# Contrast adjustment on one core: a split sixth load, and the first store moved from SyncE's queue to ScalarE's

## The chip, the cores and the metric

The kernel runs on one core of a Trainium2 chip. The metric is the time of one execution on the device in microseconds (us), lower is better. A core has five engines that run their own instruction streams: TensorE (PE in the profile), VectorE (DVE), ScalarE (ACT), GpSimd (POOL) and SyncE (SP). Data moves between the chip's memory (HBM) and the on-chip memory (SBUF, 128 partitions) by 16 DMA engines. A transfer is issued by an instruction on SyncE or ScalarE; the transfers that SyncE issues form one queue (q1 in the profile) and those that ScalarE issues another (q10), and every one of the 16 DMA engines works on both.

## The reference

The input is a batch of 16 pictures with 3 channels of 512x512 float32 values, 50.33 MB in all. Each channel picture has its own mean; values are pushed away from it by a factor of 1.5 and clipped to 0..1.

```python
batch, c, h, w = 16, 3, 512, 512
mean = np.mean(x, axis=(2, 3), keepdims=True)
return np.clip(mean + factor * (x - mean), 0, 1).astype(np.float32)
```

The formula is `factor * x + (1 - factor) * mean`, so a channel picture must be summed whole before its first value can be written.

## The kernel before

There are 48 channel pictures of 262,144 values. A picture is laid over 32 partitions of 8192 values each (`ROW`), so that a tile of 128 partitions holds four pictures and is 4.19 MB; there are 12 tiles, 0 to 11. All tiles live in a ring of `BUFS = 6` buffers, and a tile is changed in place: tile t uses buffer t modulo 6, so load t + 6 has to wait until store t has left the buffer.

For one tile the work is: one load (`load`, L63, on SyncE); `add` (L72), a copy in place on ScalarE that also sums each partition's row; `shift_by` (L77), a small matmul with a block matrix that adds the sums of 32 partitions and scales them, so that every partition holds the picture's shift in `bias`; `clip` (L83 and L87), two passes of VectorE, multiply and add, then maximum and minimum; and one store (`store`, L66), by default on ScalarE.

The order is written out by hand (`manual_schedule`): each engine takes its instructions in the order of the program, and the framework adds the waits that the data needs. It also gives every DMA one of eight semaphores, each used several times over; a DMA that takes over a semaphore may get a wait for the earlier DMA on it.

What sets the order around the change:

- SyncE issues loads 0 to 5 at once, without a wait. Then it issues store 0 in three pieces (`CUTS`: columns 0 to 1024, 1024 to 3072, 3072 to 8192), as soon as tile 0 has been clipped, then load 6 (which waits for all three pieces), load 7 (which waits for store 1), and so on to load 11.
- ScalarE sums tiles 0 to 4. Then comes a sum of the first 512 columns of tile 5 (`FIRST`), which waits until load 5 has landed. Because ScalarE works in order, this small sum is a gate: store 1 stands behind it in the program, then the sum of the other 7680 columns, then stores 2 to 4, store 5, and from there a sum and a store for each tile.
- So until load 5 has landed, no store of ScalarE's queue starts; the pieces of store 0 stand in SyncE's queue behind the six loads.

Below, "load 5" is the sixth load, "the gate" is the sum of 512 columns, and "piece 1, 2, 3" are the pieces of store 0.

Of the kernel before, what the change touches and what calls it, by code (L numbers as in the profile page):

```python
# [1 line left out]

# [4 lines left out]


P = 128  # L10
ROW = 8192
BUFS = 6
FIRST = 512
CUTS = (0, 1024, 3072, ROW)


@with_exitstack
def kernel(
    ctx: ExitStack,
    tc: tile.TileContext,  # L20
    x: bass.AP,
    factor: float,
    out: bass.AP,
):
    nc = tc.nc
    f32 = mybir.dt.float32
    Alu = mybir.AluOpType
    Act = mybir.ActivationFunctionType

    B, C, H, W = x.shape  # L30
    n_img, n_pix = B * C, H * W
    ppi = n_pix // ROW
    per_tile = P // ppi
    n_tiles = n_img // per_tile
    assert ppi * ROW == n_pix and per_tile * n_tiles == n_img and n_tiles > BUFS

    factor = float(factor)
    wconst = (1.0 - factor) / float(n_pix)

    x_f = x.rearrange("b c h w -> (b c h w)")  # L40
    out_f = out.rearrange("b c h w -> (b c h w)")

    def dram(ap, t, c0=0, c1=ROW):
        return bass.AP(tensor=ap.tensor, offset=t * P * ROW + c0, ap=[[ROW, P], [1, c1 - c0]])

    consts = ctx.enter_context(tc.tile_pool(name="consts", bufs=1))
    xpool = ctx.enter_context(tc.tile_pool(name="xpool", bufs=1))
    small = ctx.enter_context(tc.tile_pool(name="small", bufs=1))
    psum = ctx.enter_context(tc.tile_pool(name="psum", bufs=1, space=bass.MemoryType.PSUM))

    sums = small.tile([P, 2 * n_tiles], f32, name="sums")
    bias = psum.tile([P, n_tiles], f32, name="bias")


    blockw = consts.tile([P, P], f32, name="blockw")
    nc.gpsimd.memset(blockw, 0.0)  # L56
    for a in range(0, P, ppi):
        nc.gpsimd.memset(blockw[a : a + ppi, a : a + ppi], wconst)  # L58

    ring = xpool.tile([P, BUFS, ROW], f32, name="ring")  # L60

    def load(t):
        nc.sync.dma_start(out=ring[:, t % BUFS, :], in_=dram(x_f, t))  # L63

    def store(t, c0=0, c1=ROW, queue=nc.scalar):
        queue.dma_start(out=dram(out_f, t, c0, c1), in_=ring[:, t % BUFS, c0:c1])  # L66

    def add(t, c0=0, c1=ROW):
        part = ring[:, t % BUFS, c0:c1]
        k = 2 * t + (c0 > 0)  # L70
        own = sums[:, k : k + 1]
        nc.scalar.activation(out=part, in_=part, func=Act.Copy, accum_out=own)  # L72
        return own

    def shift_by(t, *parts):
        for k, part in enumerate(parts):
            nc.tensor.matmul(  # L77
                bias[:, t : t + 1], blockw, part, start=k == 0, stop=k == len(parts) - 1
            )

    def clip(t):
        part = ring[:, t % BUFS, :]
        nc.vector.tensor_scalar(  # L83
            out=part, in0=part, scalar1=factor, scalar2=bias[:, t : t + 1],
            op0=Alu.mult, op1=Alu.add,
        )
        nc.vector.tensor_scalar(  # L87
            out=part, in0=part, scalar1=0.0, scalar2=1.0, op0=Alu.max, op1=Alu.min
        )

    with tc.manual_schedule():
        for t in range(BUFS):
            load(t)

        gate = BUFS - 1
        for t in range(gate):
            shift_by(t, add(t))
            clip(t)  # L100
        for c0, c1 in zip(CUTS[:-1], CUTS[1:]):
            store(0, c0, c1, nc.sync)
        load(BUFS)
        first = add(gate, 0, FIRST)
        store(1)
        load(BUFS + 1)
        shift_by(gate, first, add(gate, FIRST))
        clip(gate)
        for t in range(2, gate):
            store(t)  # L110
            load(t + BUFS)
        for t in range(gate, n_tiles):
            if t > gate:
                shift_by(t, add(t))
                clip(t)
            store(t)
            if t + BUFS < n_tiles:
                load(t + BUFS)


# [1 line left out]
_INS = ['x', 'factor']  # L122
_OUTS = [((16, 3, 512, 512), 'float32')]

_NUMBERS = {'factor': 1.5}


# [26 lines left out]
```

## Time and profile before

| | |
|---|---|
| time, median of 3 runs | 239.94 us (239.68 to 240.33) |
| the profiled execution's own time | 239.92 us |
| its span, from the first to the last instruction | 238.1 us |
| moved by DMA | 100.66 MB, 423 GB/s over the span |
| VectorE busy | 107.0 us (45%) |
| ScalarE busy | 86.9 us (37%) |
| TensorE busy | 7.6 us (3%) |
| load 5 landed, gate ran | 62.06, 62.08 us |
| load 6 issued | 81.40 us |
| store 11 (the last) issued, landed | 220.07, 237.14 us |

The page gives the busy time of each engine, then the span in 40 slices of 5.95 us with the share in which the DMA engines were busy and the rate that they moved, then the queues, the chain of work that ended last, groups of instructions, and the DMA issues. The trace behind it has one record for each row of data that a DMA engine moved (start, duration, queue, bytes; 32,768 bytes is one partition of a whole tile, and an engine moves eight of them for a tile), and the times at which each DMA's semaphore was raised, which is what "landed" means here. Times in the text are counted from the start of the span, which is 1.8 us shorter than the execution's time.

### The profile page before, as it was taken

Reading aid. Unit: us, or ns where it says so; the run is one execution under the profiler, and the core shown is the slowest. Engines: PE = TensorE matmul, PEld = TensorE weight load, DVE = VectorE, ACT = ScalarE, POOL = GpSimd, SP = SyncE. Lnnn points to the kernel's source line nnn. Section 1 sums busy time; section 2 is a strip of 40 time slices with the busy share of each in tenths; the row PEclk is TensorE's granted clock in tenths of the full one; section 3 lists DMA queues with packets and bytes.
Section 4 is the critical chain, followed back from the end, with each engine's and each line's share of the span. In section 5 each row is a group of like instructions: output and inputs, shape, how many; then the busy total and the mean of one; then the engine's idle time right before and its main releaser. Section 6 shows DMA issues by size and latency. Waiting matters only on the chain.

```text
span 238.1 us, 209 instructions
## 1 busy us (share of the span) xinstructions
PE 7.6 (3%) x26; PEld 6.5 (3%) x26; DVE 107.0 (45%) x24; ACT 86.9 (37%) x27; POOL 0.9 (0%) x9
## 2 busy tenths in 40 slices
PE   0000000000100000000000000000000000000000
PEld 0000000000000000000000000000000000000000
DVE  0004988988979200000760490292094077059000
ACT  2085956959560000019007406503801900830000
POOL 1000000000000000000000000000000000000000
DMA  7999999999999999999999999999999999999995
GB/s 264 440 440 440 440 440 435 440 424 374 407 429 433 459 424 424 413 440 435 440 435 440 440 435 435 424 435 435 413 429 435 440 435 440 440 435 435 424 435 226
DMA packets 3744, 100.66 MB, mean 423 GB/s; under 512 B 416, under 2 KB 416, under 8 KB 544
## 3 DMA queue, kind: packets, MB, share of 16 engines
q1 hardware_dynamic: 2160, 54.53, 53.7%
q10 hardware_dynamic: 1584, 46.14, 44.9%
HBM read 50.33 MB, written 50.33 MB: 423 GB/s over the span
## 4 chain that ended last, share of the span: by engine, by line
DMA 55%; another core or an unknown queue 25%; DVE 4%; ACT 3%; issue 3%; SPq 1%; PE 0%
DMA ring<-in_x_dram 41%; DMA out_dram<-ring 15%; ACT ring L72 3%; DVE ring L83 2%; DVE ring L87 2%; SPq L63 1%; PE bias L77 0%
## 5 line engine op out<-in xcount | busy, mean ns | idle before, releaser
L72 ACT ACTIVATE ring<-ring 128x8192 f32<-128x8192 f32 (+2 forms) x13 | 84.5, 6503 | 122.7 <-DMA ring<-in_x_dram 122.7
L83 DVE TENSOR_SCALAR ring<-ring,bias 128x8192 f32<-128x8192 f32 x12 | 53.9, 4492 | 112.6 <-PE bias L77 112.6
L87 DVE TENSOR_SCALAR ring<-ring 128x8192 f32<-128x8192 f32 x12 | 53.1, 4427 | 0.4
L77 PE MATMUL bias<-sums,blockw 128*128 128x1 f32 x26 | 7.6, 360 | 203.5 <-ACT ring L72 198.8
L77 PEld LDWEIGHTS bias<-sums,blockw 128*128 128x128 f32 x26 | 6.5, 311 | 204.5 <-ACT ring L72 179.4
L72 ACT ACTIVATION_READ_ACCUMULATOR ring<-ring 128x1 f32 x13 | 2.4, 186 | 0.0
L72 ACT ACT_TABLE_LOAD x1 | 1.3, 1283 | 0.7 <-PEq L135 0.7
L58 POOL MEMSET blockw<- 32x32 f32 x4 | 0.5, 118 | 0.2
L56 POOL MEMSET blockw<- 128x128 f32 x1 | 0.2, 205 | 0.3 <-POOLq L135 0.3
L135 POOL MEMSET const-bfloat16-1.0<- 128x1 bf16 x1 | 0.1, 113 | 0.0
L135 POOL MEMSET const-uint8-127<- 128x1 uint8 x1 | 0.1, 113 | 0.0
L135 POOL MEMSET const-float32-1.0<- 128x1 f32 x1 | 0.1, 110 | 0.0
L135 POOL MEMSET const-float32-0.0<- 128x1 f32 x1 | 0.1, 104 | 0.2 <-issue 0.2
## 6 DMA issues: line engine op xcount, KB each, us to landing
ring<-in_x_dram SPq DMA_DIRECT2D x12, 4096.0 KB, 45.9
out_dram<-ring ACTq DMA_DIRECT2D x11, 4096.0 KB, 46.1
out_dram<-ring SPq DMA_DIRECT2D x1, 2560.0 KB, 50.6
out_dram<-ring SPq DMA_DIRECT2D x1, 1024.0 KB, 35.5
out_dram<-ring SPq DMA_DIRECT2D x1, 512.0 KB, 33.5
```

The costliest lines, as they stand in the source:

```text
L56: nc.gpsimd.memset(blockw, 0.0)
L58: nc.gpsimd.memset(blockw[a : a + ppi, a : a + ppi], wconst)
L63: nc.sync.dma_start(out=ring[:, t % BUFS, :], in_=dram(x_f, t))
L72: nc.scalar.activation(out=part, in_=part, func=Act.Copy, accum_out=own)
L77: nc.tensor.matmul(bias[:, t : t + 1], blockw, part, start=k == 0, stop=k == len(parts) - 1)
L83: nc.vector.tensor_scalar(out=part, in0=part, scalar1=factor, scalar2=bias[:, t : t + 1], op0=Alu.mult, op1=Alu.add,)
L87: nc.vector.tensor_scalar(out=part, in0=part, scalar1=0.0, scalar2=1.0, op0=Alu.max, op1=Alu.min)
L135: nc = _bacc.Bacc("TRN2", target_bir_lowering=False, num_devices=1)
```

## The change

The load of tile 5 becomes two DMAs, columns 0 to 6912 and columns 6912 to 8192 (`TAIL = 1280`), both on SyncE. The gate, which reads columns 0 to 512, then depends on the first part only. The three pieces of store 0 go from SyncE to ScalarE; there they stand behind the gate and ahead of store 1. SyncE goes from the loads of tile 5 directly to load 6, and all stores are on ScalarE's queue. The rest of tile 5 (columns 512 to 8192) waits for both parts.

```diff
+TAIL = 1280
 CUTS = (0, 1024, 3072, ROW)
...
-    def load(t):
-        nc.sync.dma_start(out=ring[:, t % BUFS, :], in_=dram(x_f, t))
+    def load(t, c0=0, c1=ROW):
+        nc.sync.dma_start(out=ring[:, t % BUFS, c0:c1], in_=dram(x_f, t, c0, c1))
 
-    def store(t, c0=0, c1=ROW, queue=nc.scalar):
-        queue.dma_start(out=dram(out_f, t, c0, c1), in_=ring[:, t % BUFS, c0:c1])
+    def store(t, c0=0, c1=ROW):
+        nc.scalar.dma_start(out=dram(out_f, t, c0, c1), in_=ring[:, t % BUFS, c0:c1])
...
     with tc.manual_schedule():
-        for t in range(BUFS):
-            load(t)
-
 
 
         gate = BUFS - 1
         for t in range(gate):
+            load(t)
+        load(gate, 0, ROW - TAIL)
+        load(gate, ROW - TAIL, ROW)
+
+        for t in range(gate):
             shift_by(t, add(t))
             clip(t)
+        first = add(gate, 0, FIRST)
         for c0, c1 in zip(CUTS[:-1], CUTS[1:]):
-            store(0, c0, c1, nc.sync)
+            store(0, c0, c1)
         load(BUFS)
-        first = add(gate, 0, FIRST)
         store(1)
         load(BUFS + 1)
         shift_by(gate, first, add(gate, FIRST))
```

More of the change, by code (lines that the diff above doesn't have):

```diff
@@ L91 @@
     with tc.manual_schedule():
-        for t in range(BUFS):
+        gate = BUFS - 1
+        for t in range(gate):
             load(t)
-        gate = BUFS - 1
+        load(gate, 0, ROW - TAIL)
+        load(gate, ROW - TAIL, ROW)
         for t in range(gate):
```

## The prediction, made before the changed kernel was built or run

> **What bounds the kernel now.** I read the slices of the page first:
>
> ```profile
> DMA  7999999999999999999999999999999999999995
> GB/s 264 440 440 440 440 440 435 440 424 374 407 429 433 459 424 424 413 440 435 440 435 440 440 435 435 424 435 435 413 429 435 440 435 440 440 435 435 424 435 226
> DMA packets 3744, 100.66 MB, mean 423 GB/s; under 512 B 416, under 2 KB 416, under 8 KB 544
> ```
>
> The DMA engines are busy from the first slice to the last; no engine of the core comes over 45%. So only three things can move the end: the start (264), the end (226), and the dip around 60 us (424, 374, 407), where the six loads run out and the stores begin. The change works on the dip alone.
>
> Next the DMA records of the trace. An engine moves a row of 32,768 bytes in 1.213 us, one of 20,480 in 0.761, one of 8192 in 0.309, one of 4096 in 0.158. A line through these is 0.0077 us + 0.0368 us per 1000 bytes. By it all rows of the kernel need 233.00 us on each of the 16 engines; the records add up to 234.58 us a engine, between 1.75 and 236.81 us. So there is hardly any idle time to win. The 1.58 us over the line lie at: the first rows of load 0 (0.69), the last two rows of load 5 (0.63, between 58 and 62 us), the entry of load 6 at 85 us (0.12) and what follows at 96 us (0.06); the remaining 0.08 are crumbs. A mean over engines:
>
> ```
> queue 1, data all moved      mean of 16 engines   last engine   landed
> load 4                              51.07            51.43       51.88
> load 5                              61.41            61.77       62.06
> piece 1 of store 0                  62.66            63.02       63.37
> ```
>
> Load 5 took 10.34 us after load 4 where eight rows need 9.70. The three pieces follow at once, since they had long stood behind it in the same queue:
>
> ```profile
> 0.75 2.88 SPq L63 DMA_DIRECT2D ring<-in_x_dram  x6
> 29.90 1.30 SPq L66 DMA_DIRECT2D out_dram<-ring  x3
> 81.40 74.34 SPq L63 DMA_DIRECT2D ring<-in_x_dram  x6
> ```
>
> Last ScalarE around the gate:
>
> ```profile
> 58.84 0.19 ACT L72 ACTIVATION_READ_ACCUMULATOR ring<-ring 128x1 f32 x1
> 62.08 0.63 ACT L72 ACTIVATE ring<-ring 128x512 f32<-128x512 f32 x1 [3.06 <-DMA ring<-in_x_dram]
> 62.09 1.49 ACTq L66 DMA_DIRECT2D out_dram<-ring  x2
> ```
>
> ScalarE is free from 59.03 us, the gate starts 0.02 us after load 5 has landed, and the first DMA behind it is issued 0.01 us later, while the gate still computes. So an issue behind the gate follows the landing by 0.03 us.
>
> **The change part by part**, against the profiled execution (239.92 us; the median of three is 239.94, so the sum holds for both).
>
> The split load. One more issue on SyncE, 0.37 to 0.53 us by those of loads 0 to 5, done by about 4.1 us; load 1 alone keeps the queue fed to 22 us, so it costs nothing. Eight rows an engine become 16: 8 x 0.0077 = 0.06, and a completion record of 0.01: +0.07 us on the bound.
>
> SyncE loses three issues (1.30 us at 29.90): nothing waits for SyncE there, so 0. The stall that they make at the end of load 5 goes with them, if my reading is right that the stores queued directly behind it stretch its last two rows (no other load, each with a load behind it, shows this; no run shows it alone). -0.63 us.
>
> When the first store can start now. The first part ends on the mean engine at 51.07 + 8 x 1.025 + 0.01 = 59.28 and on the last at 59.64; load 4, with a load behind it, landed 0.45 after its last engine, load 1 0.35: say 60.05. ScalarE is free (a cover of 1.0 us: if the sum of tile 4 ended later than 60.05, the gap below would grow one for one). Piece 1 is issued at 60.08. The second part ends on the mean engine at 59.28 + 8 x 0.196 + 0.01 = 60.86.
>
> From issue to first row there are three rows. At the start, with idle engines, load 0 was issued at 0.75 and its first rows began at 1.94 on average: 1.19. Store 1 was issued at 62.09 and began at 65.68 (3.6), load 6 at 81.40 and began at 85.50 (4.1), both into engines busy with the other queue. If an engine holds some 64 KB of rows already fetched (as the two stretched rows of load 5 suggest), these two become 1.1 and 1.65 us, since that much of the other queue was moved ahead of them. Piece 1 comes when only 0.8 us of small rows are left, so the start of the kernel is nearest: 1.19, first rows at 61.27, a gap of 61.27 - 60.86 = 0.41 us; 0.87 with 1.65.
>
> The first row after a gap. At the start it was stretched by 0.69 us; piece 1, following without a gap, by nothing. A queue that starts afresh is nearer to the first: +0.69, bounds 0 and 0.69.
>
> The Trainium skill, "DMA: Bandwidth & Descriptors", section "Latency and other measured facts", gives about 600 ns for the first byte of a DMA from these queues; by it the first row stands ready at 60.68, before the second part is through, and there would be no gap. The trace's own 1.19 us is what I use.
>
> ScalarE's new work. Three issues (0.348, 0.435 and 0.432 on SyncE; up to 1.06 as stores 2 and 3 took) put store 1 at 61.3 to 63.3 instead of 62.09, but its turn comes after the pieces' 1.27 + 2.47 + 6.09 = 9.8 us, near 71.8. The sum of the other columns of tile 5 moves by at most 1.6 us, its clip from 79.03 to at most 80.7; store 5 has no turn before about 144, when stores 2 to 4 are through. Cost 0.
>
> The order of transfers. Store 0 now has the engines to itself: it lands near 72.5 instead of 81.39, load 6 is issued then, and with the 4.1 us of before its rows begin at 76.4 to 76.6, not 85.50. Loads and stores then alternate, 19.4 us for a load. Store 1 has 3.8 rows out by then, the other 4.2 take 10.2 us, it lands at 88.2 (81.58 before), and load 7 is issued; load 6 keeps queue 1 fed to 95.8, so 7.6 us of cover. Were it gone, queue 10 would use the engines alone. Load 11 lands near 194 instead of 203.27, and store 11 is ready 16.8 us later, at 211, with its turn at about 226.5: 15 us of cover, 5.8 before. The bytes are the same and a row takes 1.213 us in mixed and in pure stretches, so 0. The stretches at 85 and 96 (0.18) I expect again at the new entry of load 6.
>
> Sum: +0.07 - 0.63 + 0.41 + 0.69 = +0.54, so 240.46, say 240.5 us. Bounds of the same mechanism: 0.07 - 0.63 + 0.41 = -0.15 and 0.07 - 0.63 + 0.87 + 0.69 = +1.00; and if the stretched rows remain with a small gap, 0.07 + 0.41 + 0.3 = 0.8.
>
> **The rivals.**
>
> *On time, and faster.* Piece 1's rows are ready when the second part ends on each engine: that takes an issue-to-row time of 0.78 us or less. Then 0.07 - 0.63 = -0.56, 239.36; and if load 6 now joins without the 0.18 of stretches, 239.18, which is over 0.3% faster. For it: the pieces are small rows, quick to fetch, and issue gets going while the engines are still warm. Against it: the only row with idle engines has 1.19.
>
> *Long start.* A queue that starts beside a busy one needs the 3.6 us of store 1 as such, not for what was fetched ahead. First rows at 63.7, gap 2.8, sum 0.07 - 0.63 + 2.8 = +2.3 to +2.9 with the stretch: 242.2 to 242.8. For it: both rows with a busy engine. Against: the engines are busy only 0.8 us more, and the two agree with the start's once rows fetched ahead are allowed for.
>
> *The gate opens late.* Piece 1 takes over a semaphore whose earlier DMA is the second part, and waits for its landing (61.22 + 0.42 = 61.64), or the first part lands late. The trace of before shows such waits: store 6 went out at 125.89 when load 7 had landed at 125.82, though its clip ended at 123.23. Then the first row is at 61.67 + 1.19 = 62.86, the gap 2.0, the sum 0.07 - 0.63 + 2.0 + 0.69 = +2.1: 242.0. Against: seven loads leave one of eight semaphores unused for piece 1.
>
> The Trainium skill, same page, section "Anatomy of one DMA — SWDGE (gpsimd) path", puts the fixed cost of a DMA at about 2.0 us, most of it the receipt from the target memory; with 2 us after 59.64 the gate would open at 61.64 as well, and the time would be 242.0. The trace's 0.29 to 0.45 us from last row to landing speaks against it, and I add nothing to this case for it.
>
> *Nothing.* The stretched rows have another cause and stay, and there is no gap: +0.07, 240.0. The same page, section "Issuing engines are not separate DMA queues", says that which engine issues changes nothing but issue time, which here would be this case. The trace agrees in that a row takes 1.213 us in either queue.
>
> **How the numbers follow.** 0.3% is 0.72 us, about what a measurement can tell here (the three runs span 0.65 us); slower starts at 240.66, faster below 239.22. Chances: the sum's case 0.60 (own range 239.8 to 241.0; 0.25 of it beyond 240.66), long start 0.14, late gate 0.11, on time 0.11 (0.07 beyond 239.22), nothing 0.04. Slower 0.25 + 0.14 + 0.11 = 0.50; faster 0.07; within 0.35 + 0.04 + 0.04 = 0.43. The range 239.5 to 242.3 leaves out the on-time case (0.11) and the upper half of the long start (0.07).
>
> **What would show it.** Gate near 60.07, piece 1 issued at once behind it; idle DMA engines or stretched rows between 60.9 and 62; load 5's rows at 1.025 without stretch; load 6 issued near 72.5; load 11 landed near 194; no stretch of idle DMA after that. Wrong would be: piece 1 issued after 61.5 (late gate), its first rows after 63 (long start), or before 61 (on time).

## The result, and the profile after

| | before | after |
|---|---|---|
| time, median of 5 runs | 239.94 us (239.68 to 240.33) | 241.21 us (241.02 to 241.34) |
| ratio to before, 95% interval | | 1.0053 (1.0038 to 1.0067) |
| profiled execution, its span | 239.92, 238.1 us | 241.28, 239.2 us |

The change makes the kernel slower by 1.27 us (0.53%). The forecast was 240.5 us in a range of 239.5 to 242.3, with 0.50 on slower. The direction and the range hold, but the sum behind the forecast (+0.54) is less than half of what came, and two of its terms were wrong in opposite directions.

The slices of the changed kernel's page, 5.98 us each:

```profile
DMA  7999999999999999999999999999999999999996
GB/s 263 438 438 438 438 438 438 438 397 414 438 416 351 438 427 427 438 433 416 411 427 438 438 438 438 433 433 438 427 438 438 438 438 438 433 427 405 427 433 263
```

The DMA engines are as busy as before. The deepest dip, though, is no longer the end of the loads. That was 424, 374, 407 and is now 397, 414 (slices 9 and 10) and then 438. The new one is 351, in slice 13, from 71.8 to 77.7 us. That is where load 6 joins. Before, load 6 joined at 85 us, and its slice showed 424.

ScalarE around the gate, start and duration in us (ACTq is its issuing of DMAs):

```profile
58.83 0.19 ACT L73 ACTIVATION_READ_ACCUMULATOR ring<-ring 128x1 f32 x1
60.10 0.63 ACT L73 ACTIVATE ring<-ring 128x512 f32<-128x512 f32 x1 [1.08 <-DMA ring<-in_x_dram]
60.11 1.08 ACTq L67 DMA_DIRECT2D out_dram<-ring  x2
...
61.22 1.82 ACTq L67 DMA_DIRECT2D out_dram<-ring  x2
63.09 6.61 ACT L73 ACTIVATE ring<-ring 128x7680 f32<-128x7680 f32 x1 [2.26 <-issue]
...
71.63 16.91 SPq L64 DMA_DIRECT2D ring<-in_x_dram  x2
```

The gate runs at 60.10 and piece 1 is issued at 60.11, as the change intends. The last line is SyncE's: load 6 goes out at 71.63 instead of 81.40.

The DMA records tell where the time went. I call "stretch" what a row takes beyond its length's usual time (1.213 us for 32,768 bytes), summed and divided by the 16 engines; "idle" is likewise per engine.

```
us per engine                         before    after    difference
all rows at the usual time            233.00   233.06      +0.06
stretch of the first rows (0 to 20)     0.72     0.71      -0.01
stretch, rows begun at 57 to 67.9       0.63     0.19      -0.44
idle, 57 to 70                          0        0.13      +0.1 to 0.2
stretch, rows begun at 67.9 to 130      0.19     1.65      +1.46
end of the last row, mean of engines  235.94   237.24      +1.30
end of the last row, last engine      236.80   237.84      +1.04
time outside the span                   1.79     2.03      +0.24
```

The idle of "before" comes out at -0.08, the error of this sum, so the difference lies between 0.13 and 0.21. (The time outside the span is taken from the unrounded spans, 238.13 and 239.25 us.) At the change from loads to stores the new kernel wins about 0.2 us. It then loses 1.46 us around load 6's entry. Its 1.65 us of stretch there are 1.02 on rows begun at 74 to 78, 0.43 at 86 to 90, 0.10 at 92, and crumbs. The first of these are rows of the stores, begun at 74.6 to 74.8: about 3 us after load 6 was issued, and about 2 us before its own first row (76.52). Such a row stands on all 16 engines in the changed kernel, and on three of them in the kernel before (begun at 85.4 to 85.8). Why does the same load, joining the same kind of stores, cost more than eight times as much? The experiments are about that.

### The profile page after: what moved, and what is told of

Its sections match the earlier page's. It is cut to its first block, busy times and chain, and to the rows that moved or that the text cites. A ratio compares the mean times of both kernels' runs of the same rounds, so it can differ in the third digit from the quotient of the medians.

```text
span 239.2 us, 211 instructions
## 1 busy us (share of the span) xinstructions
PE 7.6 (3%) x26; PEld 6.5 (3%) x26; DVE 107.0 (45%) x24; ACT 87.0 (36%) x27; POOL 0.9 (0%) x9
## 4 chain that ended last, share of the span: by engine, by line
DMA 51%; another core or an unknown queue 24%; DVE 4%; issue 3%; ACT 3%; SPq 1%; ACTq 1%; PE 0%
DMA ring<-in_x_dram 32%; DMA out_dram<-ring 19%; ACT ring L73 3%; DVE ring L84 2%; DVE ring L88 2%; SPq L64 1%; ACTq L67 1%; PE bias L78 0%
```

## The experiments

All kernels were timed in five rounds against the kernel before. Times are medians, with the ratio to the kernel before and its 95% interval. Stretch, idle time and the times of rows are those of one profiled execution of each kernel. The medians of the kernel before in the three series were 239.81, 239.73 and 239.63 us.

### First series: the moment, or engines in lockstep?

Two theories. M, the moment: load 6 now joins earlier (near 76 instead of 85), alone and while VectorE works on tile 5. L, lockstep: the short idle gap lets all engines begin the pieces within 0.2 us of each other (0.6 us apart in the kernel before), so that load 6 hits all of them at once.

**Load 6 into buffer 1.**

```diff
+    def slot(t):
+        return {BUFS: 1, BUFS + 1: 0}.get(t, t % BUFS)
-        ... ring[:, t % BUFS, ...]
+        ... ring[:, slot(t), ...]
```

> The changed kernel, but load 6 goes into buffer 1 and load 7 into buffer 0, so that load 6 waits for store 1 instead of store 0. It should be issued near 81 us, with load 7 directly behind it, as in the kernel before, and not at 71.6. In the changed kernel the rows around load 6's entry were stretched by 1.55 us a engine (1.02 at 74 to 78 us, 0.43 at 86 to 90, 0.10 at 92); in the kernel before by 0.18. Theory M (the moment: load 6 joins store 1 early, alone, while VectorE clips tile 5): the stretches fall to about 0.2 and the time to 241.2 - 1.35 = 239.85 us. Theory L (lockstep: the short idle gap at 61 us makes all 16 engines start the pieces together, so that load 6's first rows meet on all of them): the stretches stay near 1.5 wherever load 6 joins, and the time at 241.2.

Measured: 240.32 us (ratio 1.0022, 1.0014 to 1.0031). This is not the experiment that I meant. Load 6 stands ahead of store 1 in the program, so with buffer 1 it did not wait for store 1 but overwrote tile 1 (which this kernel therefore never stores). SyncE issued it at 39.50 us, long before the gate, so that it followed load 5 without a pause:

```profile
39.50 42.37 SPq L67 DMA_DIRECT2D ring<-in_x_dram  x2
```

As a kernel with seven loads ahead of the stores it still says something. The rows at the end of load 5 were not stretched and no engine idled. The pieces began at 64.3 us beside load 6, whose last rows, at 68 to 71 us, were stretched by 0.4; about 0.5 came from 85 us on, where load 7 joins. The proper version is in the third series.

**A longer second part.**

```diff
-TAIL = 1280
+TAIL = 2048
```

> The changed kernel with the second part of load 5 at 2048 columns instead of 1280. The gate opens near 59.2 us and piece 1's rows come near 60.1, while the second part is still being moved, so no engine idles and the engines keep the 0.6 us by which their rows are apart. Theory L: load 6's entry costs about 0.2 and the time is near 239.7 to 239.9 us. Theory M: the entry still costs 1.5; only the gap of 0.2 goes: 241.0.

Measured: 241.85 us (1.0068, 1.005 to 1.0086). The gate in this kernel:

```profile
59.21 0.63 ACT L73 ACTIVATE ring<-ring 128x512 f32<-128x512 f32 x1 [0.19 <-DMA ring<-in_x_dram]
59.22 0.86 ACTq L67 DMA_DIRECT2D out_dram<-ring  x2
```

Both theories missed the time. The gate opened at 59.21 and no engine idled, yet the later stretch is 1.69. So the gap is not needed, and L as I had put it falls. The engines are less in step than in the changed kernel, but more than in the kernel before: at load 6's entry the rows of 14 of the 16 begin within 0.29 us (0.15 and 0.41). I come back to this below. The rest of the loss in the profiled execution (242.19 us) is two engines that end at 238.57 and 238.78, where the mean of the 16 is 236.91.

**The kernel before, store 4 first on ScalarE.**

```diff
         load(BUFS)
         first = add(gate, 0, FIRST)
+        store(4)
         store(1)
...
         for t in range(2, gate):
-            store(t)
+            if t != 4:
+                store(t)
             load(t + BUFS)
```

> The kernel before, but ScalarE issues store 4 first (it has to wait for its clip, 68.65 us), then stores 1, 2, 3. The pieces of store 0, still behind load 5 on SyncE's queue, then have the engines to themselves, store 0 lands near 72 instead of 81.4, and load 6 joins near 76 us beside store 4, with no idle gap at 61 us before. Theory M: the entry costs about 1.5 as in the changed kernel, and the time is 239.94 + 1.35 = 241.3 us. Theory L: the engines were never idle, the entry costs 0.2, and the time stays at 239.9.

Measured: 239.69 us (0.9999, 0.9988 to 1.001). The slices of this kernel, 5.95 us each, and from its timeline SyncE's issue of load 6:

```profile
GB/s 265 441 441 441 441 435 441 424 419 408 393 466 408 419 419 441 441 441 435 435 435 441 435 419 419 424 435 441 441 435 435 435 435 430 430 441 408 430 441 265
```

```profile
71.86 0.34 SPq L63 DMA_DIRECT2D ring<-in_x_dram  x1
```

Load 6 was issued at 71.86 us and its first rows began at 75.89, as early as in the changed kernel. Slices 12 and 13 together carry (466 + 408) / 2 = 437, with no hole (466 is more than the engines move anywhere else; rows seem to be booked in the slice where they begin, so the two are read together). The stretch at the entry is 0.07. An early entry alone costs nothing, so M as the mere moment falls. What was left of it was VectorE, which stood idle from 68.7 to 77.0 us here.

**The changed kernel without the split.**

```diff
-        load(gate, 0, ROW - TAIL)
-        load(gate, ROW - TAIL, ROW)
+        load(gate)
```

> The changed kernel without the split: load 5 is one DMA again, the gate waits for all of it, and the pieces are on ScalarE. The gate opens 1.57 us after where it did against the end of the load: landing near 61.6 us, piece 1's rows 0.9 us later near 62.5, idle 1.6 us more than in the changed kernel. Both theories: 241.2 + 1.5 = 242.7 us. The last two rows of load 5 on each engine should not be stretched (0.63 us in the kernel before), since no store stands behind them in the queue; if they are, the stretch has another cause and the time is 243.3.

Measured: 242.93 us (1.0128, 1.0113 to 1.0144); 242.7 was expected. Slices of this kernel, 6.04 us each:

```profile
GB/s 260 434 434 434 434 434 434 434 434 434 311 432 385 412 390 407 428 434 434 434 434 434 434 434 434 434 434 434 434 434 434 434 434 434 434 434 434 434 434 184
```

The move alone costs 3.1 us; 311 is the idle gap. The engines idle 1.69 us, and the later stretch is 1.62. The rows of load 5 take 1.217 us on average, so they are not stretched: the 0.63 us of the kernel before do come from stores that wait behind the load.

### Second series: VectorE, or a queue that has gone empty?

Theory V: VectorE's passes over tile 5, at 70 to 79 us, hinder the entry. Theory Q: SyncE's queue had stood empty for 15 us, and a queue that starts afresh costs this.

**No clip of tile 5.**

```diff
         shift_by(gate, first, add(gate, FIRST))
-        clip(gate)
```

> The changed kernel without the two VectorE passes on tile 5 (that part of the computation is left out; all transfers stay). VectorE is then idle from 68.7 us until tile 6 is summed, so nothing but DMA runs when load 6 joins near 76 us. The runs so far: with VectorE's clip of tile 5 running at the entry, the rows were stretched by 1.02, 0.81 and 1.09 us at 74 to 79 us; in the run with store 4 first, load 6 joined as early, but VectorE was idle then, and the stretch was 0.07. Theory V (VectorE's passes hinder the entry): the first stretch falls from 1.02 to about 0.1 and the time from 241.2 to 240.2 us, or to 239.8 if the second stretch at 86 to 92 (0.53) goes too. Theory Q (SyncE's queue had been empty for 15 us, and a queue that starts afresh costs this whatever the engines do; with store 4 first it had been empty for 4 us): stretches and time stay, 241.2.

Measured: 241.10 us (1.0059, 1.0047 to 1.0071). Slices of this kernel:

```profile
GB/s 263 438 438 438 438 438 438 438 397 417 435 417 356 433 395 428 438 438 428 417 438 438 438 438 438 433 438 433 428 438 433 422 428 438 433 428 422 438 438 263
```

VectorE does nothing from 68.4 us until tile 6 has landed and been summed, and slice 13 still drops to 356 and slice 15 to 395. V falls.

**The clip of tile 5 later.**

```diff
-        shift_by(gate, first, add(gate, FIRST))
-        clip(gate)
         for t in range(2, gate):
             store(t)
             load(t + BUFS)
+        shift_by(gate, first, add(gate, FIRST))
+        clip(gate)
```

> The changed kernel, but the sum of tile 5's other columns and its clip stand behind stores 2 to 4, so that the sum starts when store 4 has been issued (68.7 us), ends near 75.5 and the clip runs from 76 to 85 us; all work is done. Theory V: load 6 is issued at 71.6, its first rows are fetched before 76, the first stretch is nearly gone, and the time is 239.9 to 240.2. Theory Q: no change, 241.2.

Measured: 241.04 us (1.0053, 1.004 to 1.0066). VectorE's rows in this kernel:

```profile
64.32 4.43 DVE L88 TENSOR_SCALAR ring<-ring 128x8192 f32<-128x8192 f32 x1
76.53 4.49 DVE L84 TENSOR_SCALAR ring<-ring,bias 128x8192 f32<-128x8192 f32 x1 [7.79 <-PE bias L78]
```

The stretched rows begin at 74.68, when VectorE has been idle for 6 us. The later stretch is 1.89. V falls again.

**The kernel before, store 4 first, with the clip of tile 5 beside the entry.** The edit is shown against the kernel with store 4 first.

```diff
+        shift_by(gate, first, add(gate, FIRST))
+        clip(gate)
         store(4)
         store(1)
         load(BUFS + 1)
-        shift_by(gate, first, add(gate, FIRST))
-        clip(gate)
```

> The kernel before with store 4 first, as in the run that took 239.69 us, but with the sum of tile 5 and its clip ahead of store 4 in the program, so that VectorE clips tile 5 from 70 to 79 us, beside the entry of load 6 at 76. Theory V: the entry costs about 1 us instead of 0.07, time 240.7. Theory Q: the queue had pieces until 71.5, the entry costs nothing, time 239.7.

Measured: 240.39 us (1.0018, 1.0007 to 1.003), between the two. The single times lie from 239.46 to 240.75, and the profile is of an execution of 239.86, so it does not show what the slower ones lose: seven of the twelve took 240.38 or more, the other five 239.86 or less. VectorE's rows in it:

```profile
70.23 4.49 DVE L83 TENSOR_SCALAR ring<-ring,bias 128x8192 f32<-128x8192 f32 x1 [1.67 <-PE bias L77]
74.76 4.43 DVE L87 TENSOR_SCALAR ring<-ring 128x8192 f32<-128x8192 f32 x1
```

VectorE worked all through the entry at 75.88 us, and not one row there was stretched; 0.36 came later, at 84 to 90.

**SyncE's queue kept in use.**

```diff
-    def store(t, c0=0, c1=ROW):
-        nc.scalar.dma_start(out=dram(out_f, t, c0, c1), in_=ring[:, t % BUFS, c0:c1])
+    def store(t, c0=0, c1=ROW, queue=nc.scalar):
+        queue.dma_start(out=dram(out_f, t, c0, c1), in_=ring[:, t % BUFS, c0:c1])
...
+        store(4, 0, FIRST, nc.sync)
         load(BUFS)
...
-            store(t)
+            store(t, FIRST if t == 4 else 0, ROW)
```

> The changed kernel, but the first 512 columns of store 4 (0.26 MB) go out on SyncE's queue ahead of load 6, as soon as tile 4 is clipped (68.65 us), and ScalarE's store 4 has the other columns. SyncE's queue has then been in use a few us before load 6 joins. Theory Q: the small store's entry may cost something, but load 6's entry falls to about 0.1, and the time to 240.0 to 240.5. Theory V: the entry costs its 1.0, the second stretch remains, 241.2.

Measured: 241.87 us (1.0088, 1.0073 to 1.0104). SyncE's issues, the small store and then loads 6 and 7:

```profile
68.67 0.35 SPq L67 DMA_DIRECT2D out_dram<-ring  x1
71.53 10.63 SPq L64 DMA_DIRECT2D ring<-in_x_dram  x2
```

The small store was under way on SyncE's queue until 81.5 us with load 6 standing behind it. When load 6 joined at 84.5, the rows at 82 to 87 were still stretched by 1.2 us. The queue had moved nothing for 3 us instead of 15, and the price is nearly the same: Q falls.

### Third series: how the stores began

Sorted by stretch, the kernels so far fell into two groups (the one with seven loads ahead left aside), and the groups differ in one thing: whether the first stores stood queued while rows of the loads were still to be moved, or came when the loads' rows had gone or were just going. Theory S says that it is this, wherever load 6 joins. Theory K says that it is the queue on which the pieces stand.

**The split alone.**

```diff
+TAIL = 1280
...
-        for t in range(BUFS):
+        for t in range(BUFS - 1):
             load(t)
+        load(BUFS - 1, 0, ROW - TAIL)
+        load(BUFS - 1, ROW - TAIL, ROW)
```

> The kernel before with the split alone: load 5 in parts of 6912 and 1280 columns, the gate on the first part, the pieces of store 0 still on SyncE's queue directly behind the loads. Store 1 is issued at 60.1 instead of 62.09 us. The split itself costs 0.07; the stretch of 0.63 at the end of the loads should stay, since stores stand behind them in the queue, and load 6 joins near 85 at 0.2. Both theories: 239.9 + 0.1 = 240.0 us.

Measured: 240.97 us (1.007, 1.0048 to 1.0093), against 240.0 expected. The six times are 239.60, 240.89, 240.93, 241.01, 241.94 and 242.31, and the profile is of the fastest. It shows 0.82 us of stretch at the end of the loads and none later, as the first group has it, though load 6 was issued only at 88.93 us and joined at 92.96. What the others lose, 1.3 to 2.7 us more, no profile here shows. At the median the split alone thus costs 1.34 us against the kernel before, as much as the whole change, and both theories had 0.1: whether its usual execution belongs to the first group is not known.

**Load 6 behind store 1, properly.** The exchange of buffers as above, and:

```diff
-        load(BUFS)
         store(1)
+        load(BUFS)
         load(BUFS + 1)
```

> The changed kernel with buffers 0 and 1 exchanged for tiles 6 and 7 and load 6 behind store 1 in the program, so that load 6 really waits for store 1: issued near 81.3 us with load 7 directly behind it, joining near 85.4 with VectorE idle, as in the kernel before. Theory S (stores that begin on their own behind the loads, on ScalarE's queue, run with little fetched ahead, so a load that joins them stretches the rows whenever it comes): the stretches stay at 1.2 to 1.6, time 241.0 to 241.3. If it were the moment alone: 0.2, time 239.8.

Measured: 241.14 us (1.0064, 1.0049 to 1.0078). Slices of this kernel, and from its timeline SyncE's issue of loads 6 and 7:

```profile
GB/s 263 439 439 439 439 439 439 439 397 409 443 417 439 439 351 433 378 422 433 439 439 439 439 439 439 439 433 433 433 439 428 422 417 433 422 439 439 439 439 263
```

```profile
81.26 1.63 SPq L67 DMA_DIRECT2D ring<-in_x_dram  x2
```

With load 6 issued when it was in the kernel before, load 7 directly behind it and VectorE idle, the hole of 351 has only moved, to slice 15 (83.7 to 89.7 us), and the second one (378) with it. The cost goes with the load's entry whenever that comes, as S says.

**The pieces on SyncE's queue, but held until the gate.** The edit is again shown against the kernel with store 4 first.

```diff
+        first = add(gate, 0, FIRST)
+        held = ring[:, 0, 0:1]
+        nc.scalar.activation(out=held, in_=held, func=Act.Copy)
         for c0, c1 in zip(CUTS[:-1], CUTS[1:]):
             store(0, c0, c1, nc.sync)
         load(BUFS)
-        first = add(gate, 0, FIRST)
         store(4)
```

> The kernel before with store 4 first (239.69 us, load 6's entry 0.07), but the pieces of store 0, still on SyncE's queue, are held until ScalarE's gate: after the gate ScalarE copies one column of tile 0 onto itself, and the pieces wait for that. They are issued near 62.6 us, so the engines idle about 2.7 us, and nothing stands behind load 5 in the queue, so its rows are not stretched (0.63 less). Theory S (it is the start on their own after a gap): load 6's entry costs 1 to 1.5, time 239.7 + 2.7 - 0.6 + 1.3 = 243.1 us. Theory K (it is that the pieces are on ScalarE's queue, ahead of the other stores): the entry costs 0.1, time 241.8.

Measured: 243.73 us (1.0167, 1.0152 to 1.0183). Slices of this kernel (6.04 us each), and from its timeline SyncE's issue of the pieces:

```profile
GB/s 260 434 434 434 434 434 434 434 434 434 217 430 481 336 401 434 434 434 434 434 434 434 418 434 434 428 423 434 434 428 434 434 434 428 434 434 434 434 434 260
```

```profile
62.48 1.65 SPq L66 DMA_DIRECT2D out_dram<-ring  x3
```

217 is the idle gap (2.51 us). Then, at load 6's entry near 80 us, there are 336 and 401. This is the kernel whose entry cost 0.07; the one thing changed in the program is that the pieces begin after the loads, still on SyncE's queue, and the later stretch is 1.67. S holds and K falls. One thing more goes with the new start, though: the engines are in step. At load 6's entry the rows of 14 of the 16 begin within 0.11 us of each other, with store 4 first within 0.43.

**The pieces begun early, on ScalarE's queue.**

```diff
-TAIL = 1280
+TAIL = 4096
...
-        for t in range(gate):
+        for t in range(gate - 1):
             shift_by(t, add(t))
             clip(t)
         first = add(gate, 0, FIRST)
         for c0, c1 in zip(CUTS[:-1], CUTS[1:]):
             store(0, c0, c1)
         load(BUFS)
+        shift_by(gate - 1, add(gate - 1))
+        clip(gate - 1)
```

> The changed kernel with the second part of load 5 at 4096 columns, and the gate and the pieces ahead of tile 4's sum, so that the gate opens near 56.7 us and the pieces begin near 57.7, some 3 us before the loads are through. No idle gap and no stores behind a load in its own queue. Theory S: the stores have begun beside the loads, load 6's entry costs 0.2, and neither the 0.63 of the kernel before nor the gap is left: 239.4 to 239.6 us, a little faster than both kernels. Theory K: the entry costs 1.5 as in the changed kernel: 240.8 to 241.0.

Measured: 240.43 us (1.0029, 1.0019 to 1.0039), between the two and 0.8 above what S had. The gate in this kernel, and its slices (5.96 us each):

```profile
56.70 0.63 ACT L73 ACTIVATE ring<-ring 128x512 f32<-128x512 f32 x1 [7.48 <-DMA ring<-in_x_dram]
56.70 0.86 ACTq L67 DMA_DIRECT2D out_dram<-ring  x2
```

```profile
GB/s 264 440 440 440 440 440 440 434 393 404 410 469 412 434 412 434 418 434 440 440 440 423 434 440 440 434 429 434 418 434 423 440 440 440 423 434 440 440 440 203
```

The pieces were issued from 56.70 us, and their first rows came at 60.49. Load 6 joined at 75.8; slices 12 and 13 together carry (469 + 412) / 2 = 440, with no hole. The later stretch fell to 0.32, from 1.65 in the changed kernel, as S says and K denies. But the last rows of the loads were stretched by 0.52, which I had expected to be gone: with stores waiting, it comes on either queue. The mean engine ends at 236.08, as in the kernel before (235.94). The rest of the loss in the profiled execution is the last engine (237.06 against 236.80) and 0.23 us outside the span.

### What the records say together

```
us per engine            idle   stretch at      stretch later   mean end   profiled
                         57-70  57 to 67.9      67.9 to 130     of rows    execution
stores wait while loads are moved
  before                  0       0.63            0.19          235.94     239.92
  store 4 first           0       0.62            0.17          235.96     239.59
  store 4 first, clip     0       0.72            0.36          236.28     239.86
  split alone             0       0.82            0.00          236.30     239.60
  begun early             0       0.52            0.32          236.08     240.46
stores come as the loads end
  after                   0.13    0.19            1.65          237.24     241.28
  second part 2048        0       0.05            1.69          236.91     242.19
  no clip                 0       0.17            1.76          237.29     241.16
  clip later              0.14    0.18            1.89          237.63     241.79
  queue kept in use       0.12    0.18            1.48          237.13     241.40
  load 6 behind store 1   0.03    0.19            1.75          237.29     241.10
  without the split       1.69    0.16            1.62          238.66     243.69
  pieces held, SyncE      2.51    0.13            1.67          239.65     243.49
```

None of these 13 profiled executions lies between the groups. The kernel with seven loads ahead is not in the table, since its loads end 10 us later; with about 0.4 us at the end of its loads and 0.5 later it stands beside the first group, a little outside the ranges below.

Where stores wait while the loads' rows are still being moved, the last rows of the loads are stretched by 0.5 to 0.8 us, and a load that joins later pays 0 to 0.4. Where they come only as the loads end, nearly nothing is stretched there, and the load that joins later pays 1.5 to 1.9, at whatever time it joins, on whichever queue the pieces are, and with or without VectorE. That the later price follows from how the stores began is shown, most plainly by holding the pieces on the same queue and by beginning them early on the other. It is not enough that stores are issued before the loads are through: with 2048 columns they were issued from 59.22 us and the last row of the loads ended at 61.23, 2.0 us later, and that was too late; issued from 56.70, 5.2 us before the last row, they were in the first group.

What in the start decides is less sure. The step of the engines, how close together their rows begin, goes with the groups too. In the second group the rows of 14 of the 16 engines begin within 0.11 to 0.15 us when the load joins, in the first within 0.41 to 0.57, and the two plainest experiments change the step along with the start (0.43 to 0.11 us by holding the pieces, 0.15 to 0.47 by beginning them early). Only two kernels break this: the split alone (0.28 us, later stretch 0.00) and the second part of 2048 columns (0.29 us, later stretch 1.69). With the same step they lie in different groups, which speaks against the step as the cause, but it is one profile each, and the first is that of an unusually quick execution, 1.3 us below the next of its kernel. So the step as the link between the start and the later price is not ruled out.

Why an engine pays at one of two places is not shown either. A guess that fits is that an engine fetches rows some way ahead of writing them, and that this lead is made either while stores wait behind loads or when the next load joins. No record here separates fetching from writing, so that stays open.

## Why the prediction was right, and where not

- The bound and the stage. Right: DMA engines with next to no idle time, all engines of the core under 46%, and the difference made by stretched rows and a gap in the stretch where stores take over.
- The split's own cost, 0.07. Right as far as the rows go: 0.06 by the usual row times, and the first part's rows took 1.029 us (1.025 expected). As a price of the split alone it was wrong: that kernel lost 1.34 us at the median, and its one profile does not show where.
- The 0.63 us at the end of the loads goes. Right in size: without a store behind it (no split) the load's rows take 1.217 us. The cause was half right: it takes stores that wait, but not in the load's own queue, since with the pieces begun early on the other queue the stretch was 0.52.
- The gate and the issue. Right: 60.10 and 60.11 against 60.07 and 60.08. The late gate did not come, since piece 1 got the unused semaphore. The first part landed at 60.08, 0.44 us after its last row, inside the 0.29 to 0.45 that the forecast used. That range holds for loads that run without stores beside them: loads 6 and 7 of the kernel before landed 1.55 and 1.56 us after their last rows. The Trainium skill's 2.0 us, "DMA: Bandwidth & Descriptors", section "Anatomy of one DMA — SWDGE (gpsimd) path", are stated for DMAs that GpSimd issues, and this one was issued by SyncE.
- From issue to first row: taken as 1.19, measured 60.11 to 60.99 = 0.88 to the first engine's row, and about 0.95 as a mean of the engines, which the 1.19 was. The gap is 0.1 to 0.2 instead of 0.41. The "on time" rival needed 0.78 or less. The Trainium skill, "DMA: Bandwidth & Descriptors", section "Latency and other measured facts", gives about 600 ns for the first byte; the measured 0.88 lies between that and the start of the kernel.
- The first row after a gap, +0.69: wrong. The first rows of piece 1 took their usual time; 0.19 us is spread over the pieces. At the change itself the kernel therefore gained 0.63 less 0.07, 0.19 and the idle of 0.1 to 0.2, so about 0.2 us, where the sum had a loss of 0.54. Here the "on time" rival was the better one.
- "The stretches at 85 and 96 (0.18) I expect again at the new entry of load 6": the step that failed. The place was named, and the size was 1.65 instead of 0.19. I took it from the kernel before as if it belonged to the load that joins. The runs show that it follows from how the stores began, which the change alters.
- "The bytes are the same and a row takes 1.213 us in mixed and in pure stretches, so 0": right for settled stretches, but the way into a mix is not free.
- The order of transfers. Right in every time: load 6 issued at 71.63 (72.5 forecast), load 7 at 88.21 (88.2), load 11 landed at 194.64 (194), store 11 ready at 211.45 (211), its first row at 227.28 (226.5). None of its covers ran out.
- The "nothing" rival was that it is all one which queue a store is on. Of the queue itself that is what the runs show: with a gap, the later stretch is 1.62 with the pieces on ScalarE's queue and 1.67 on SyncE's. This agrees with the section of the same page of the Trainium skill, "Issuing engines are not separate DMA queues", by which transfers run on the same 16 DMA engines whichever engine started them. The time changed because the start of the stores did.
- Not foreseen at all: 0.24 us more outside the span.

The likeliest case's own range (239.8 to 241.0) missed by 0.2 us; the wide range held. That it held, and that the direction did, is in part luck. The loss that was expected at the change (0.54) did not come, and a loss of 1.46 us that the sum did not have did: two errors of opposite sign that partly cancelled. The 0.50 on slower was made up of the gap with its stretched first rows, the long start and the late gate, and none of these is what made the kernel slower.

## What to carry to other kernels

When DMA is the bound and never idle, look at the single rows: time is lost as rows that take longer, at the points where the mix of loads and stores changes, and in these kernels the price followed from the way that the stores were started, not from the transfer on which it showed. Stores queued behind the loads before these were through cost 0.5 to 0.8 us once; holding them back until the loads ended made that cost nearly vanish, and 1.5 to 1.9 us came back, from 13 to 23 us later. When a kernel's single times lie far apart, as with the split alone, the profile of one execution may not show what the median pays. A term that is read off the old kernel as "will happen again" deserves its bounds as much as one that is new.

## What the runs showed of the hardware that was not expected

- The price of a change from stores alone to stores and loads was 0 to 0.4 us (0.5 with seven loads ahead) or 1.5 to 1.9 us, and nothing between in the profiled executions, by how the stores had begun.
- A second DMA queue beside a busy one needed 3.6 us from issue to first row (store 1 in the kernel before) and 3.8 when the pieces were begun early (56.70 to 60.49), but 0.88 when the rows ahead were small and nearly through.
- All nine profiled executions with the pieces on ScalarE's queue had 2.01 to 2.12 us outside the span; the five with the pieces on SyncE's queue had 1.78 to 1.79. The cause was not looked for.
- With the second part at 2048 columns two engines ended 1.7 and 1.9 us after the mean of the 16; the time is that of the last.
